# A one-core hybrid layer: low-rank decay products from the two rounded parts of x, GLA states kept in DRAM, 29 row buffers, and no head start for the RWKV pairs on TensorE

## The chip, the core and the metric

The kernel runs on one core of one Trainium2 chip. A core has TensorE (PE, matrix products), VectorE (DVE), ScalarE (ACT) and GpSimd (POOL) for elementwise work, and SyncE (SP), whose queue issues all DMAs of this kernel. The engines run their own instruction streams in order and wait for one another through semaphores. The metric is the device time of one execution in microseconds.

## What is computed

One inference step of one layer. `x` holds 1024 prompt tokens and 8 sample tokens of width 1024. One wide projection `p = x w_in` feeds three branches.

- GLA, four heads with key width 128 and value width 256. Its decay comes from a product of low rank: `a_lr` is a 16-column slice of `p`, and

```python
log_a = log_sigmoid(a_lr @ gla_alpha_w2 + gla_alpha_b) / 16
S_t = diag(a_t) S_{t-1} + k_t^T v_t ;  o_t = q_t S_t
```

- RWKV-7, sixteen heads of width 64, a recurrence with a rank-one correction per token, done in chunks of 64 tokens.
- Two sigmoid gates that weigh `o_gla @ w_up_gla` and `o_rwkv @ w_up_rwkv`. Their sum goes through `w_out`, a residual and a layer norm.

New states of both recurrences are outputs too. All inputs are fp32.

## The kernel before

**Two passes.** Prompt tokens are worked off in two halves (`PASS`). Pass 0 has 512 prompt tokens and the 8 sample tokens, as two column tiles of 260. Pass 1 has 512 tokens in one tile of 512. In each pass x is held transposed, as eight tiles of 128 rows of the width (k = 0 to 7).

**Products of three parts.** TensorE multiplies numbers of the type float32r, which are fp32 values rounded to fewer bits, faster than fp32. So x and every weight are split into a rounded part and the rounded rest: `xh`, `xl` (by `load_x`: a DMA into a row buffer, a rounding copy on ACT, a subtraction on DVE or POOL) and `whi`, `wlo` (by `load_w`). Each product of a weight block is three float32r matmuls per k: `xh whi`, `xl whi`, `xh wlo`, accumulated in one PSUM bank (`blocks`). There is one `xh` and one `xl` buffer per k, so that pass 1's parts overwrite pass 0's when the last block of pass 0 has used them.

**The low-rank product** (`low_rank`, stream kind "rank") is different: it multiplies the unrounded x rows (`raws`) by the 16 columns `wa` in fp32, with k = 0 to 7 spread over three groups of 16 output columns at 0, 32 and 64, which are added up afterwards. Raw rows are freed only when it has read them. Its result is split into three 16-row pieces of `alr` (one such tile per pass), against which `gla_head` multiplies `gw2`.

**GLA heads** (`gla_head`, kind "head"). Each works through four chunks of 128 tokens with a state `S`. Pass 0's last state of each head stays in an SBUF tile `GS` and is read by pass 1.

**RWKV pairs** (`pair`, eight per pass, kinds "pair", "turn", "chain", "norm"). The front of a pair computes decays, keys and the in-chunk matrices; a small triangular inverse is done on DVE in 31 steps, whose operand comes back from DRAM in another layout (`LD`, `Lp`, loaded as `wide<-LD`); the chain runs through 8 chunks: `pr` (`pch<-wide,gg`) to DVE (`rh`), `pu` (`pch<-rh,XT`) to ACT, `pS` (`pch<-wide`) to DVE, and so on; the norm ends it with sums over heads (`big<-part,headsr`).

**What sets the order.** Nothing is ordered at run time. A planner (class `Order`) records every operation from many coroutines: it takes, again and again, the operation with the smallest key. The key is the time at which its model lets the operation start, less a bonus: `PRIO` by stream kind off TensorE, `ON_PE` by stream kind on TensorE.

```python
key = t - (s.on_pe if s.op.eng == "P" else s.prio)
```

Where two can start at the same time, the stream with the higher `PRIO` goes first; the blocks of the projection ("block") have 0. In the model a PE operation that reads what DVE, ACT or POOL writes starts no earlier than a margin (`HOP` plus `SPARE`) after it. Each engine then executes its recorded list in order. Since one helper records every operation, all rows of the profile carry its line, L216, and are told apart by tile names. Pass 1 gets its `whi` and `wlo` back from DRAM copies (`whi<-wh`, `wlo<-wl`) through the four buffers of each kind.

**Row buffers.** 26 buffers of 128 x 520 fp32 ("row") serve x rows, projections and most temporaries.

Of the kernel before, what the change touches and what calls it, by code (L numbers as in the profile page):

```python
# [10 lines left out]
F32 = mybir.dt.float32  # L11
F32R = mybir.dt.float32r
# [8 lines left out]
P = 128  # L21
D = 1024
NK = D // P
# [12 lines left out]
NGC = HT // GC  # L36
# [8 lines left out]
HALF = HT + NS  # L45
SBUF = {
    "row": ([P, HALF], 26), "wide": ([P, 2 * HT], 4), "gg": ([P, 4 * HT], 2), "lw": ([P, HT], 2),
    "l2s": ([P, 2 * P], 1), "pc": ([P, NCH], 3), "X": ([P, 256], 1),
# [28 lines left out]
        "head": 0.3, "gate": 0.05, "w": 0.3, "out": -0.1, "state": 0, "block": 0.0}  # L77
ON_PE = {"evacuate": 0.0, "pair": 0.15, "turn": 0.1, "chain": 0.15, "norm": 0.15, "x": 0.0, "lora": 0.15, "rank": 0.1,
         "head": 0.1, "gate": 0.06, "w": 0.0, "out": -0.03, "state": 0.1, "block": 0.0}
# [64 lines left out]
def price(eng, name, out, args, ins):  # L144

    n = out.free_size()
    src = [x for x in ins if x.tensor.space != PSUM] if eng == "A" else ins
    if eng == "P":
        m = args[0].free_size()
        rows, cols = tiles(name, args)  # L150
        if name == "transpose":
            return 0.112
        if args[0].dtype == F32R:
            return max(m / 1200, n / 2200) if rows == cols == P else (m + n) / 1200
        if rows == cols == P:
            return 2 * max(m, n) / 1200 + 0.005
        return 2 * (m + n) / 1200 * rows * cols / P ** 2
# [5 lines left out]
    wide = max([n, *(x.free_size() for x in ins)]) if name in ("tensor_reduce", "bn_stats", "bn_aggr") else n  # L163
# [240 lines left out]
class Kern(Order):  # L404
# [71 lines left out]
    def setup(self):  # L476
# [80 lines left out]
    def load_constants(self):  # L557
        a, V, E = self.a, self.V, self.E
        yield from self.load("wa", self.S.dma_start(self.wa, a["wa"]))
        self.has.add("wa")  # L560
        row = yield from self.row()
        yield V.memset(row, 1.0)
        yield V.tensor_copy(self.onesr, row[:, :P])
        yield V.memset(row, 0.0)
        for t in self.alr:
            yield V.tensor_copy(t, row[0:96])
        self.has.add("alr")
        yield from self.load("pv", self.S.dma_start(self.pv, a["pv"]))
# [10 lines left out]
        yield self.S.dma_start(heads, a["heads"])  # L579
        for n in range(3):  # L580
            yield self.S.dma_start(raw[32 * n:32 * n + 16], a["gla_alpha_w2"])
        yield self.S.dma_start(self.lev, a["lev"])
# [7 lines left out]
    def load_x(self, src, i, wait=None, low_rank=False):  # L590
# [3 lines left out]
        base, n = PASS[i][:2]  # L594
        raws, his, xs, used = [], [], [], [NK]
        self.xq.append(xs)
        if low_rank:
            used = [0]
            self.spawn(self.low_rank(self.ctx[i], raws, used), "rank")

# [77 lines left out]
    def blocks(self):  # L678
        xs = None
        for b in self.plan:  # L680
# [12 lines left out]
            for tt, (t0, n) in enumerate(tiles):  # L693
# [3 lines left out]
                for k in range(NK):  # L697
# [23 lines left out]

    def low_rank(self, c, raws, used):

        ps = []
        for t0, n in c.tiles:
            ps.append((yield from self.bank("big", [P, n])))
        for k3 in range(0, NK, 3):
            ks = range(k3, min(NK, k3 + 3))
            yield lambda: len(raws) > ks[-1] and "wa" in self.has
            for (t0, n), q in zip(c.tiles, ps):  # L730
                for k in ks:
                    g = 32 * (k - k3)
                    yield self.P.matmul(q[g:g + 16], self.wa[:, 16 * k:16 * k + 16], raws[k][:, t0:t0 + n],
                                            start=(k < 3), stop=(k + 3 >= NK))
            used[0] = ks[-1] + 1
        x_ = yield from self.row(c.n)
        for (t0, n), q in zip(c.tiles, ps):
            x = x_[0:16, t0:t0 + n]
            yield self.C.copy(x, q[0:16])
            for g in (32, 64):  # L740
                yield self.V.tensor_add(x, x, q[g:g + 16])
            self.free(q)

            hi, lo, hi2 = (self.alr[c.i][g:g + 16, t0:t0 + n] for g in (0, 32, 64))
            yield lambda: "alr" in self.has
            yield self.C.copy(hi, x)
            yield self.C.copy(hi2, x)
            yield self.V.tensor_sub(lo, x, hi.bitcast(F32))
            c.alr_ready += 1
        self.free(x_)  # L750

# [18 lines left out]
    def gla_head(self, c, h, rows, g):  # L770
# [7 lines left out]
        for t0, w in c.tiles:  # L778
            pz = yield from self.bank("big", [P, w])
            yield self.P.matmul(pz, self.gw2[:, h * GDK:(h + 1) * GDK], self.alr[c.i][:, t0:t0 + w], start=True, stop=True)  # L780
            yield A.activation(z[:, t0:t0 + w], pz, AF.Identity, bias=self.pvec("gab", h))
            self.free(pz)
        yield A.activation(al, z, AF.Abs)
        yield A.activation(al, al, AF.Exp, scale=-1.0)
# [56 lines left out]

        S = self.GS[h] if c.i else None

# [11 lines left out]
        for x in range(NGC):  # L855
# [9 lines left out]
            for j in range(2):  # L865
                yield A.copy(v[j][:, s], po[:, j])
            Sn = self.GS[h] if x == NGC - 1 else (yield from self.get("S"))
            if S is not None:
                yield V.scalar_tensor_tensor(Sn, S, tot[:, x:x + 1], pS, ALU.mult, ALU.add)
                if x:  # L870
                    self.free(S)
            else:
                yield V.tensor_copy(Sn, pS)
            self.free(pb)
            S, VK = Sn, VKn
        if c.i:
            yield S_.dma_start(self.o["gla_p"][0, 0, h], S)
        else:
            yield from self.gla_sample(h, q, k, v, al, [(AT_, z), (km_, vk1)], qp_)
# [737 lines left out]
    def run_all(self):  # L1617
# [6 lines left out]
        self.ctx = [SimpleNamespace(i=i, base=b, n=n, ns=ns, tiles=t, gla_done=0, rwkv_done=0, fronts=0, lw_ready=False,  # L1624
                                    alr_ready=0, merged=0, half=0, gated=0,
                                    rg=[[] for _ in range(NPAIR)], gg=[[] for _ in range(GH)])
# [61 lines left out]
```

## Time and profile before

| what | value |
|---|---|
| median of 3 runs | 1630.18 us (1628.06 to 1632.21) |
| the profiled execution | 1629.18 us, span 1627.4 us |
| TensorE busy | 1579.8 us, 97% of the span |
| weight loads on TensorE (PEld) | 1394.6 us, 86% |
| VectorE busy | 1226.9 us, 75% |
| ScalarE busy | 844.6 us, 52% |
| GpSimd busy | 92.3 us, 6% |
| DMA | 318.42 MB, 62.9% of the 16 engines' span |

In a row of the profile stand the engine, the operation, what it writes `<-` what it reads, its shape, how often it occurs (xN), and after a bar its busy time in us and the mean of one in ns; then the idle time of the engine ahead of it and what ended that. A row of the timeline has the start and the length in us ahead of it. fp32 matmuls leave two records each, float32r matmuls one. Matmul rows overlap, since matmuls are pipelined; the distance from start to start is what one costs in a stream.

### The profile page before, as it was taken

What the parts mean: (1) busy time and instruction counts of PE and PEld (TensorE: products, weight loads), DVE (VectorE), ACT (ScalarE), POOL (GpSimd) and SP (SyncE); (2) the same over time, 40 slices, a digit from 0 to 9 for tenths busy, and PEclk for the clock granted to TensorE, in tenths of its full rate; (3) what the DMA queues carried; (4) which work ended last, traced back from release to release, by engine and by line L of the source; (5) the groups of instructions that cost most, each with busy time, mean ns of one, the idle gap of its engine ahead of it and who ended that gap; (6) DMA issues with size and microseconds to landing.
All of it is one profiled execution on the core that took longest, in us unless ns stands there. A gap on an engine that the chain in (4) does not pass through costs nothing.

```text
span 1627.4 us, 29876 instructions
## 1 busy us (share of the span) xinstructions
PE 1579.8 (97%) x10066; PEld 1394.6 (86%) x10066; DVE 1226.9 (75%) x3201; ACT 844.6 (52%) x2054; POOL 92.3 (6%) x185
## 2 busy tenths in 40 slices
PE   8999999999999999999999999999999999999998
PEld 7899999989999998788877887788788889977786
DVE  6786897788888887678677987898676784666555
ACT  5446765656566656463625472446354555554210
POOL 1100000101010000000100011100000000000000
PEclk9999999999999999999999999999999999999999
DMA  9877785696568765754465546544654487789432
GB/s 291 254 228 235 219 263 174 188 285 207 168 199 284 220 205 173 235 166 131 149 187 156 149 148 208 178 115 150 188 156 132 139 251 226 253 276 289 155 111 84
DMA packets 339572, 318.42 MB, mean 196 GB/s; under 512 B 103011, under 2 KB 225004, under 8 KB 339420
## 3 DMA queue, kind: packets, MB, share of 16 engines
q1 hardware_dynamic: 339420, 316.52, 62.9%
q8 instruction: 80, 1.31, 0.4%
q14 instruction: 72, 0.59, 0.1%
HBM read 197.55 MB, written 117.82 MB: 194 GB/s over the span
## 4 chain that ended last, share of the span: by engine, by line
PE 71%; DVE 12%; DMA 6%; SPq 4%; ACT 3%; issue 2%; POOL 0%; POOLq 0%; DVEq 0%; ACTq 0%
PE proj L216 41%; PE big L216 20%; PE pY L216 6%; SPq L216 4%; PE pch L216 4%; DVE row L216 4%; DVE X L216 2%; DVE wide L216 2%; DVE Xt L216 1%; DMA wide<-LD 1%; ACT row L216 1%; DMA wlo<-wl 1%; DVE wlo L216 1%; DMA row<-xT 1%; DMA row<-o_gla 1%
## 5 line engine op out<-in xcount | busy, mean ns | idle before, releaser
L216 PE MATMUL proj<-xh,whi 128*128 128x260 f32 (+1 forms) x1872 | 617.3, 330 | 3.8 <-DMA whi<-wh 3.1
L216 PE MATMUL proj<-xh,wlo 128*128 128x260 f32 (+1 forms) x1872 | 617.0, 330 | 1.5 <-DMA wlo<-wl 1.0
L216 PE MATMUL proj<-xl,whi 128*128 128x260 f32 (+1 forms) x1872 | 616.7, 329 | 0.0
L216 PEld LDWEIGHTS proj<-xh,whi 128*128 128x128 f32 x1872 | 355.5, 190 | 29.9 <-issue 4.6
L216 PEld LDWEIGHTS proj<-xh,wlo 128*128 128x128 f32 x1872 | 355.3, 190 | 28.7 <-issue 3.0
L216 PEld LDWEIGHTS proj<-xl,whi 128*128 128x128 f32 x1872 | 355.4, 190 | 23.3 <-issue 2.5
L216 ACT CAST whi<-wraw 128x512 fp32r<-128x512 f32 x210 | 130.0, 621 | 100.1 <-PE proj L216 51.5
L216 DVE TENSOR_TENSOR row<-row 128x512 f32<-128x512 f32 (+9 forms) x334 | 164.1, 498 | 11.7 <-ACT row L216 4.2
L216 DVE TENSOR_TENSOR wlo<-wraw,whi 128x512 fp32r<-128x512 f32 x205 | 141.3, 692 | 39.4 <-ACT whi L216 35.8
L216 ACT ACTIVATE row<-row 128x512 f32<-128x512 f32 (+4 forms) x229 | 138.1, 610 | 38.1 <-DVE row L216 28.7
L216 DVE TENSOR_TENSOR Xt<-X,wide 128x60 f32<-128x60 f32 (+24 forms) x496 | 105.1, 212 | 43.2 <-DMA wide<-LD 32.4
L216 ACT ACTIVATE row<-proj,omu 128x260 f32<-128x260 f32 (+1 forms) x99 | 54.3, 548 | 137.9 <-PE proj L216 137.2
L216 PE MATMUL big<-row 128*128 128x64 f32 (+4 forms) x712 | 115.9, 280 | 2.8 <-DVE row L216 1.8
L216 DVE TENSOR_TENSOR X<-X,Xt 128x60 f32<-128x60 f32 (+24 forms) x496 | 105.0, 212 | 12.5
L216 ACT ACTIVATE s0p<-wide,pc 64x64 f32<-64x64 f32 x256 | 87.9, 343 | 41.7 <-DVE wide L216 37.7
L216 PEld LDWEIGHTS big<-row 128*128 128x128 f32 (+1 forms) x712 | 98.1, 192 | 12.5 <-DVE row L216 4.6
L216 ACT COPY wide<-pch 64x64 f32<-64x64 f32 x216 | 44.6, 207 | 97.5 <-PE pch L216 94.2
L216 DVE SCALAR_TENSOR_TENSOR wide<-pch,pc,s0p 64x64 f32<-64x64 f32 x224 | 63.0, 281 | 42.7 <-PE pch L216 38.5
L216 DVE SCALAR_TENSOR_TENSOR row<-proj,pv,row 128x259 f32<-128x259 f32 (+1 forms) x99 | 56.4, 570 | 42.3 <-ACT tail L216 28.7
L216 ACT COPY row<-big 128x128 f32<-128x128 f32 (+7 forms) x161 | 46.0, 309 | 68.0 <-PE big L216 66.7
L216 POOL TENSOR_TENSOR row<-row 128x512 f32<-128x512 f32 (+5 forms) x35 | 38.2, 1092 | 580.7 <-ACT row L216 188.7
L216 PE MATMUL big<-az,wide 128*128 128x256 f32 x256 | 65.9, 382 | 0.3 <-ACT wide L216 0.2
(255 smaller groups left out, 2647.4 us busy)
## 6 DMA issues: line engine op xcount, KB each, us to landing
wraw<-w_in SPq DMA_DIRECT2D x146, 256.0 KB
wh<-whi SPq DMA_DIRECT2D x146, 256.0 KB
wl<-wlo SPq DMA_DIRECT2D x146, 256.0 KB
whi<-wh SPq DMA_DIRECT2D x146, 256.0 KB
wlo<-wl SPq DMA_DIRECT2D x146, 256.0 KB
wide<-LD SPq DMA_DIRECT2D x64, 128.0 KB
wraw<-w_up_gla SPq DMA_DIRECT2D x32, 256.0 KB
wraw<-w_up_rwkv SPq DMA_DIRECT2D x32, 256.0 KB
```

What stands on the lines that cost most here:

```text
L216: ways.append((eng, lambda call=call: call(out, *args, **kw), price(eng, name, out, args, ins)))
```

## The change

1. **Low-rank product.** `wa` is split once into `war`, a float32r tile with 32 columns per k: 16 of the rounded part and 16 of the rest. For each k and column tile two float32r matmuls run: `xh` against all 32 columns and `xl` against the first 16. There is one group of output columns, so the three-way addition goes. It no longer reads raw rows, which are freed as soon as `xl` is made. In pass 1 it may start only when all four heads of pass 0 have read `alr` (one tile for both passes now). `xh`, `xl` of a pass are freed by the pass's last block only once the low-rank product is recorded (`ranked`).
2. **GLA states.** `GS` is four DRAM tiles. Pass 0 writes each head's last state there, and pass 1 loads it into an `S` buffer: 4 stores and 4 loads of 128 KB more on SP.
3. **Buffers.** "row" has 29 buffers in place of 26.
4. **Planner.** `ON_PE` of "pair", "turn", "chain" and "norm" goes from 0.15, 0.1, 0.15, 0.15 to 0, and the planner's price of a float32r matmul with few columns is that of a full one.

Two constants' work differs: `gla_alpha_w2` is loaded six times instead of three, and two `alr` clearings fall away.

```diff
-    "row": ([P, HALF], 26), "wide": ([P, 2 * HT], 4), ...
+    "row": ([P, HALF], 29), "wide": ([P, 2 * HT], 4), ...
-ON_PE = {"evacuate": 0.0, "pair": 0.15, "turn": 0.1, "chain": 0.15, "norm": 0.15, "x": 0.0, ...
+ON_PE = {"evacuate": 0.0, "pair": 0.0, "turn": 0.0, "chain": 0.0, "norm": 0.0, "x": 0.0, ...
         if args[0].dtype == F32R:
-            return max(m / 1200, n / 2200) if rows == cols == P else (m + n) / 1200
+            return max(m / 1200, n / 2200) if rows == P else (m + n) / 1200
...
-        self.wa = cp.tile([P, NK * 16], F32, name="wa")
-        self.alr = [cp.tile([96, HALF], F32R, name=f"alr{n}") for n in range(2)]
+        self.war = cp.tile([P, NK * 32], F32R, name="war")
+        self.alr = cp.tile([96, HALF], F32R, name="alr")
-        self.GS = [cp.tile([P, GDV], F32, name=f"GS{h}") for h in range(GH)]
+        self.GS = [self.dr.tile([P, GDV], F32, name=f"GS{h}") for h in range(GH)]
...
+        yield V.tensor_copy(wa[:, :, 0:16], raw)
+        yield V.tensor_sub(wa[:, :, 16:32], raw, wa[:, :, 0:16].bitcast(F32))
...
-                yield lambda: used[0] > k
                 self.free(raws[k])
...
                     if fin and b.last:
+                        yield lambda: b.c.ranked
                         self.free(xh, xl)
...
-    def low_rank(self, c, raws, used):
+    def low_rank(self, c, xs):
+        yield lambda: c.i == 0 or self.ctx[0].decays == GH
         ps = []
         for t0, n in c.tiles:
             ps.append((yield from self.bank("big", [P, n])))
-        for k3 in range(0, NK, 3):
-            ks = range(k3, min(NK, k3 + 3))
-            yield lambda: len(raws) > ks[-1] and "wa" in self.has
+        for k in range(NK):
+            yield lambda: len(xs) > k and "wa" in self.has
             for (t0, n), q in zip(c.tiles, ps):
-                for k in ks:
-                    g = 32 * (k - k3)
-                    yield self.P.matmul(q[g:g + 16], self.wa[:, 16 * k:16 * k + 16], raws[k][:, t0:t0 + n],
-                                            start=(k < 3), stop=(k + 3 >= NK))
+                for x, m in list(zip(xs[k], (32, 16)))[::-1 if k else 1]:
+                    yield self.P.matmul(q[0:m], self.war[:, 32 * k:32 * k + m], x[:, t0:t0 + n],
+                                        start=(k == 0 and m == 32), stop=(k == NK - 1 and m == 32))
+        c.ranked = True
...
-        S = self.GS[h] if c.i else None
+        S = None
+        if c.i:
+            S = yield from self.get("S")
+            yield S_.dma_start(S, self.GS[h])
...
-            Sn = self.GS[h] if x == NGC - 1 else (yield from self.get("S"))
+            Sn = yield from self.get("S")
...
+        yield S_.dma_start(self.o["gla_p"][0, 0, h] if c.i else self.GS[h], S)
+        self.free(S)
```

The planner's table moves instructions on every engine. Three places are shown as they stand in the recorded lists.

**PE, pass 1, the fourth chunk of the sixth chain.** `pch<-wide,gg` is the product `pr`, whose result DVE copies to `rh`; `pch<-rh,XT` is `pu`, which waits for that copy; the `proj` rows are the projection. Before:

```order
L216 MATMUL pY<-gg,wide 128x128
L216 MATMUL pch<-wide,gg 128x128
L216 MATMUL pY<-az_177,wide 128x128
L216 MATMUL proj<-xl_9744,whi 128x512
L216 MATMUL proj<-xh_9703,wlo 128x512
L216 MATMUL proj<-xh_9712,whi 128x512
L216 MATMUL pch<-rh,XT_181 128x128
```

Now:

```order
L216 MATMUL pY<-gg,wide 128x128
L216 MATMUL pch<-wide,gg 128x128
L216 MATMUL pY<-az_176,wide 128x128
L216 MATMUL proj<-xh_9722,wlo 128x512
L216 MATMUL proj<-xh_9729,whi 128x512
L216 MATMUL proj<-xl_9731,whi 128x512
L216 MATMUL proj<-xh_9729,wlo 128x512
L216 MATMUL pch<-rh,XT_180 128x128
```

One more projection matmul stands between the two products of the chain.

**SP, pass 1, ahead of the weight block `4624`** (its first load is `whi<-wh4624_0`; `LD`, `Lp` and `wide` are the fourth pair's transfers through DRAM, `o_gla` and `sg` stores). Before:

```order
L216 DMA o_gla_90<-row_12062 128x512
L216 DMA LD13_13074<-gg_12689 32x8x32 x4
L216 DMA Lp0_184<-gg_12689 32x4x32 x4
L216 DMA wide_12688<-LD13_13074 32x1024
L216 DMA sg107_115<-row_13125 128x512
L216 DMA wide_12688<-LD13_13074 32x1024 x3
L216 DMA whi_13091<-wh4624_0_4726 128x512
L216 DMA wlo_13092<-wl4624_0_4779 128x512
```

Now:

```order
L216 DMA o_gla_90<-row_12063 128x512
L216 DMA LD13_13054<-gg_12682 32x8x32 x4
L216 DMA Lp0_183<-gg_12682 32x4x32 x4
L216 DMA wide_12681<-LD13_13054 32x1024 x4
L216 DMA whi_13088<-wh4624_0_4686 128x512
L216 DMA sg107_115<-row_13135 128x512
L216 DMA wlo_13089<-wl4624_0_4690 128x512
```

The store `sg107` stood ahead of `whi` and now stands behind it.

**PE, at the turn from pass 0 to pass 1** (blocks of 260 columns are pass 0's last, those of 512 pass 1's first; `row` is a raw x row). Before:

```order
L216 MATMUL proj_9650<-xl7_314,whi_9457 128x260
L216 MATMUL proj_9650<-xh7_285,wlo_9491 128x260
L216 MATMUL proj_9715<-xh0_9658,whi_9558 128x512
L216 MATMUL proj_9715<-xl0_9660,whi_9558 128x512
L216 MATMUL big_9266<-row_9662,wa_143 16x512
L216 MATMUL proj_9715<-xh0_9658,wlo_9559 128x512
L216 MATMUL proj_9715<-xh1_9667,whi_9558 128x512
```

Now:

```order
L216 MATMUL proj_9619<-xh4_248,wlo_9439 128x260
L216 MATMUL big_9230<-xl1_9645,war_143 16x512
L216 MATMUL big_9230<-xh1_9643,war_143 32x512
L216 MATMUL big_9230<-xl2_9654,war_143 16x512
L216 MATMUL big_9230<-xh2_9652,war_143 32x512
L216 MATMUL big_9230<-xl3_9667,war_143 16x512
L216 MATMUL big_9230<-xh3_9663,war_143 32x512
```

The low-rank matmuls of pass 1 read the split parts, and ten of the sixteen (k = 0 to 4) stand inside pass 0's last block.

More of the change, by code (lines that the diff above doesn't have):

```diff
@@ L46 @@
 SBUF = {
-    "row": ([P, HALF], 26), "wide": ([P, 2 * HT], 4), "gg": ([P, 4 * HT], 2), "lw": ([P, HT], 2),
+    "row": ([P, HALF], 29), "wide": ([P, 2 * HT], 4), "gg": ([P, 4 * HT], 2), "lw": ([P, HT], 2),
     "l2s": ([P, 2 * P], 1), "pc": ([P, NCH], 3), "X": ([P, 256], 1),
@@ L77 @@
         "head": 0.3, "gate": 0.05, "w": 0.3, "out": -0.1, "state": 0, "block": 0.0}
-ON_PE = {"evacuate": 0.0, "pair": 0.15, "turn": 0.1, "chain": 0.15, "norm": 0.15, "x": 0.0, "lora": 0.15, "rank": 0.1,
+ON_PE = {"evacuate": 0.0, "pair": 0.0, "turn": 0.0, "chain": 0.0, "norm": 0.0, "x": 0.0, "lora": 0.15, "rank": 0.1,
          "head": 0.1, "gate": 0.06, "w": 0.0, "out": -0.03, "state": 0.1, "block": 0.0}
@@ L558, in load_constants @@
         a, V, E = self.a, self.V, self.E
-        yield from self.load("wa", self.S.dma_start(self.wa, a["wa"]))
+        row = yield from self.row()
+        raw = row[:, :NK * 16]
+        yield from self.load("wa", self.S.dma_start(raw, a["wa"]))
+        wa, raw = (x.rearrange("p (k c) -> p k c", k=NK) for x in (self.war, raw))
+        yield V.tensor_copy(wa[:, :, 0:16], raw)
+        yield V.tensor_sub(wa[:, :, 16:32], raw, wa[:, :, 0:16].bitcast(F32))
         self.has.add("wa")
-        row = yield from self.row()
         yield V.memset(row, 1.0)
         yield V.tensor_copy(self.onesr, row[:, :P])
[L564 to L567, printed above, removed]
         yield from self.load("pv", self.S.dma_start(self.pv, a["pv"]))
@@ L579, in load_constants @@
         yield self.S.dma_start(heads, a["heads"])
-        for n in range(3):
-            yield self.S.dma_start(raw[32 * n:32 * n + 16], a["gla_alpha_w2"])
+        for n in range(6):
+            yield self.S.dma_start(raw[16 * n:16 * n + 16], a["gla_alpha_w2"])
         yield self.S.dma_start(self.lev, a["lev"])
@@ L726, in low_rank @@
             ps.append((yield from self.bank("big", [P, n])))
-        for k3 in range(0, NK, 3):
-            ks = range(k3, min(NK, k3 + 3))
-            yield lambda: len(raws) > ks[-1] and "wa" in self.has
+        for k in range(NK):
+            yield lambda: len(xs) > k and "wa" in self.has
             for (t0, n), q in zip(c.tiles, ps):
-                for k in ks:
-                    g = 32 * (k - k3)
-                    yield self.P.matmul(q[g:g + 16], self.wa[:, 16 * k:16 * k + 16], raws[k][:, t0:t0 + n],
-                                            start=(k < 3), stop=(k + 3 >= NK))
-            used[0] = ks[-1] + 1
-        x_ = yield from self.row(c.n)
+                for x, m in list(zip(xs[k], (32, 16)))[::-1 if k else 1]:
+                    yield self.P.matmul(q[0:m], self.war[:, 32 * k:32 * k + m], x[:, t0:t0 + n],
+                                        start=(k == 0 and m == 32), stop=(k == NK - 1 and m == 32))
+        c.ranked = True
         for (t0, n), q in zip(c.tiles, ps):
[L738 to L741, printed above, removed]
+            hi, lo, hi2 = (self.alr[g:g + 32, t0:t0 + n] for g in (0, 32, 64))
+            yield self.C.copy(hi, q[0:32])
+            yield self.C.copy(hi2, q[0:32])
+            yield self.V.tensor_sub(lo, q[0:32], hi.bitcast(F32))
             self.free(q)
[L744 to L748, printed above, removed]
             c.alr_ready += 1
-        self.free(x_)
     def landing(self, c, rows, tt):
@@ L779, in gla_head @@
             pz = yield from self.bank("big", [P, w])
-            yield self.P.matmul(pz, self.gw2[:, h * GDK:(h + 1) * GDK], self.alr[c.i][:, t0:t0 + w], start=True, stop=True)
+            yield self.P.matmul(pz, self.gw2[:, h * GDK:(h + 1) * GDK], self.alr[:, t0:t0 + w], start=True, stop=True)
             yield A.activation(z[:, t0:t0 + w], pz, AF.Identity, bias=self.pvec("gab", h))
             self.free(pz)
+        c.decays += 1
         yield A.activation(al, z, AF.Abs)
```

14 lines of the change are left out of this document (5 added, 9 removed).

## The prediction

> **What bounds the kernel now.** I read the page's busy times and the chain of waits first, then what TensorE (PE) waits for, then the timeline and the windows at the places that the change moves.
>
> ```profile
> span 1627.4 us, 29876 instructions
> PE 1579.8 (97%) x10066; PEld 1394.6 (86%) x10066; DVE 1226.9 (75%) x3201; ACT 844.6 (52%) x2054; POOL 92.3 (6%) x185
> PE 71%; DVE 12%; DMA 6%; SPq 4%; ACT 3%; issue 2%; POOL 0%; POOLq 0%; DVEq 0%; ACTq 0%
> 14.02 19.54 PE proj L216 x160
> 1435.51 5.59 PE pY L216 x24
> ```
>
> PE sets the time: it is busy in 97% of the span and holds 71% of the chain. The last two rows are unbroken stretches of the chain, and give my unit prices: 160 matmuls of 260 columns in 19.54 us are 0.122 each, 24 of 512 columns in 5.59 us are 0.233 each. Most of those 1579.8 us can't be touched, since the matmul count hardly changes. What can change is what PE loses beyond these spacings, in waits and in a lowered clock. The view of waits gives the wait on each releaser as total, times and longest:
>
> ```profile
> PE pch L216 <- DVE wide L216: 6.2, 7, 2.0
> PE pch L216 <- DVE rh L216: 4.5, 5, 1.5
> PE big L216 <- DVE part L216: 3.2, 7, 0.9
> PE proj L216 <- DMA whi<-wh: 3.1, 2, 2.5
> PE big L216 <- DMA row<-xT: 7.1, 3, 4.0
> ```
>
> The first three are short results of DVE in the RWKV chains and norms that come late; the last two are DMAs.
>
> **The sum's base.** The profiled execution took 1629.2 us, span 1627.4 and 1.8 around it. It lies 1.0 under the median of 1630.2, so I add 1.0 at the end.
>
> **A, the low-rank product of pass 1.** The pass needs eight fp32 products of 16 x 512 before and sixteen float32r ones after.
>
> ```profile
> 632.50 0.28 PE L216 MATMUL proj<-xh,wlo 128*128 128x260 f32 x1
> 632.71 1.03 PE L216 MATMUL big<-row,wa 128*16 128x512 f32 x2
> 633.67 0.49 PE L216 MATMUL pch<-rh,XT 128*128 128x128 f32 x2
> ```
>
> Start to start, one fp32 product took 0.96 (632.71 to 633.67), so eight take 7.7. Sixteen of float32r at 0.233 take 3.7. Entering the narrow product cost 0.09 (632.50 to 632.71 is 0.21 in place of the 0.12 of a 260-column row); with three or four entries that is 0.3, together 4.0: **-3.7**. No row shows float32r with a 16- or 32-column stationary. The bounds are the row of full width, 0.233, and half of the fp32 row, one of its two passes, 0.48. The second makes 7.7 and a gain of nothing. I take the first: the float32r row is of the same type and length of stream.
>
> The Trainium skill, "TensorEngine Tiling (Array Packing)", Key Properties, says that a change of tiling mode drains TensorE; that speaks against a product now strewn in more pieces. The trace has it at 0.09 an entry; some twelve entries in both passes would be 1.1 us, against about ten before, so by row and rule alike the sum keeps its value within 0.2.
>
> **B, the start.** In pass 0 the fp32 products lie in the first projection block, which waits for loads anyway.
>
> ```profile
> 9.70 0.42 PE L216 MATMUL proj<-xh,whi 128*128 128x260 f32 x1
> 9.92 0.42 PE L216 MATMUL proj<-xl,whi 128*128 128x260 f32 x1
> 11.13 1.11 PE L216 MATMUL big<-row,wa 128*16 128x260 f32 x12
> 12.18 0.39 PE L216 MATMUL proj<-xh,whi 128*128 128x260 f32 x1
> 12.97 1.05 PE L216 MATMUL big<-row,wa 128*16 128x260 f32 x6
> 13.95 0.39 PE L216 MATMUL proj<-xh,wlo 128*128 128x260 f32 x1
> 12.09 0.69 DVE L216 TENSOR_TENSOR xl<-row,xh 128x520 fp32r<-128x520 f32 x1
> ```
>
> Only 1.05 (11.13 to 12.18) and 0.98 (12.97 to 13.95) show as time, 2.0 together. Now 32 float32r products of 260 columns stand there, 3.9 at 0.122, partly at the start's slow pace of 0.22 (9.70 to 9.92). They too can fill waits, since the last `xl` is made only at 12.78. I take 3.9 less 1.1 of cover less 2.0: **+0.8**; bounds -1.5 (all covered but 0.5) and +2 (none covered).
>
> **C, the turn of the passes.** The columns of the window's row are length, then busy time and count of PE, PEld, DVE, ACT and POOL, the granted clock, the DMA share and GB/s.
>
> ```profile
> 666.00:673.00 7.00, 7.00 (x18) 3.82 (x17) 5.70 (x18) 2.38 (x5) 0.00 (x0) 0.55 0.69 259
> 665.80 1.09 PE L216 MATMUL big<-row,wa 128*16 128x512 f32 x2 [2.03 <-DMA row<-xT]
> 659.86 5.90 DMA row<-xT
> ```
>
> PE stood 2.03 us for an x row and then ran 7 us at a granted clock of 0.55, which loses 0.45 x 7 = 3.1; together 5. After the change the order shows ten low-rank matmuls of k = 0 to 4 inside pass 0's last block and the raw rows freed earlier, into three more buffers, so the x loads can start earlier. A part x7 still needs its DMA (5.90), cast and subtraction. By the order, the work on PE between the release of a buffer and the first use of its x is 6.0 to 10 us for k = 4 to 7: close, so I keep a wait of 2 without the slow clock: **-3**. Bounds: -5 (all gone) and +3 (the wait grows by the 1.4 us of cast and subtraction, and a clock loss like this one's half more).
>
> The Trainium skill, "TensorE: Matmul & The Clock Gate", Part 1, has the clock halve after an idle window of about 3.4 us. Here the granted clock fell behind a recorded wait of 2.03, and the measurement decides: by the rule a kept wait of 2 would cost only itself as it did before, C would be 0, and the sum 1620.8.
>
> **D, the chains.** Without the head start of 0.15 the products `pr` and `pu` are recorded when the model has them ready, with more of the projection between.
>
> ```profile
> 1206.71 0.39 PE L216 MATMUL pch<-wide,gg 128*128 128x128 f32 x2
> 1207.08 0.48 PE L216 MATMUL proj<-xl,whi 128*128 128x512 f32 x1
> 1208.40 0.19 DVE L216 TENSOR_TENSOR Xt<-X,wide 128x31 f32<-128x31 f32 x1 [2.27 <-DMA wide<-LD]
> 1208.62 0.29 DVE L216 COPY rh<-pch 128x128 f32<-128x128 f32 x1
> 1208.97 0.49 PE L216 MATMUL pch<-rh,XT 128*128 128x128 f32 x2 [0.95 <-DVE rh L216]
> ```
>
> This is the place that the order shows: DVE stood 2.27 us for the inverse's operand from DRAM, its copy `rh` queued behind it, and PE waited 0.95. One more matmul between (0.233) takes that much of such a wait away, not all. Over all chains, my count of the recorded lists at these spacings: `pr` to `pu` had under 1.0 us of other work in 52 of 128 steps, now in none; `pS` to the next `pr` under 1.1 us in 55 of 240, now in 13. The two rows of `pch` waits are 10.7 us; some 2 us more hides in starts that are late by less than a row shows, about 13. Ends that come from DVE standing for a DMA stay. I take some 40%: **-5**, bounds -10 (three quarters) and 0. If PE's other work is now what ends late, the price shows as longer chains, and a chain behind delays pass 1's last norms only.
>
> **E, fronts and norms.** `part` to `headsr` had under 1 us of work in 11 cases, now 3; products on `az` under 1.5 us in 26, now 10. Their waits are the `part` row, 3.2, and some 2 of smaller ones: **-2**, bounds -5 and 0.
>
> **F, a weight load behind a store.** The order on SP shows `sg107` passing from ahead of `whi` to behind it.
>
> ```profile
> 984.56 1.80 SPq L216 DMA_DIRECT2D LD<-gg  x4
> 986.40 3.26 SPq L216 DMA_DIRECT2D Lp<-gg  x4
> 990.33 0.42 SPq L216 DMA_DIRECT2D sg<-row  x1
> 992.25 0.37 SPq L216 DMA_DIRECT2D whi<-wh  x1
> 992.25 4.12 DMA whi<-wh
> 993.62 0.40 PE L216 MATMUL proj<-xh,wlo 128*128 128x512 f32 x1
> 996.50 0.47 PE L216 MATMUL proj<-xh,whi 128*128 128x512 f32 x1 [2.49 <-DMA whi<-wh]
> 996.00:1003.00 7.00, 6.50 (x21) 4.94 (x22) 5.68 (x26) 0.00 (x0) 0.00 (x0) 0.76 1.01 360
> ```
>
> The load was issued at 992.25, behind thirteen other issues, landed 4.12 later, and PE stood 2.49 and ran at 0.76 for 7 us: 0.24 x 7 = 1.7, together 4.2. After the change the weight load has 4.7 us or more of PE work between its issue and its use, more than it takes to land: **-3.5**, bounds -4.2 and 0. A planner's new order makes such places elsewhere, too; I put one half of this one against it: **+2**, bounds 0 and +6 (one such place and a half).
>
> **G, the states from DRAM.** Four stores and four loads of 128 KB are new. The stores hide, as nothing waits for them before pass 1. Each load stands on SP right behind two weight loads, whose buffers a PE matmul frees; from that matmul to the first read of `S` stand 27 to 31 matmuls of mixed size, 5.5 to 6.4 us by the spacings. The nearest DMAs have the same 128 KB:
>
> ```profile
> 181.48 4.82 DMA l2s<-lora
> 1171.64 2.60 DMA l2s<-lora
> 38.28 0.61 SPq L216 DMA_DIRECT2D l2s<-lora  x1
> 46.08 0.29 DVE L216 CAST l2p<-l2s 128x256 fp32r<-128x256 f32 x1
> ```
>
> With two issues of 0.37 ahead, a landing of 2.60 or 4.82 arrives by 3.3 to 5.6, in time; the earliest load took 7.8 to its use, and would be late by 2 to 3. DVE reads `S` and PE only its result. **+2**, bounds 0 and +22 (all four late, below).
>
> **The sum.** -3.7 + 0.8 - 3 - 5 - 2 - 3.5 + 2 + 2 = -12.4. So 1616.8 for an execution like the profiled one, and with the 1.0, **1617.8 us**.
>
> **Rivals.**
>
> *R1, the waits only change place.* The chain waits end when DVE is done, and DVE is late since it stands for `wide<-LD`, which the change leaves; the DMA waits of C and F come up at other places. For it: the 2.27 above. Against: slack grew at most edges. Left are A and B, -2.9: **1627.3**.
>
> *R2, narrow float32r products cost what an fp32 pass costs.* Then A is 0, and B is 32 x 0.24 = 7.7 in place of 3.9, +3.8: **1625.3**. For it: no row has this form. Against: the fp32 row is of another type.
>
> *R3, slower: PE stands for the `S` loads.* The states' products follow `S` at once. It decides from a landing of about 5 us; at 7.8 PE waits 7.8 + 0.7 - 6 = 2.5, and a clock as low as in C's window adds 3.1. Four times 5.6 is 22.4 in place of G's 2: **1638.2**. For it: the load at 38.28, and the DMA share of 0.69 and 1.01 in the two windows shown. Against: the 2.60 and 4.82.
>
> **How the numbers follow.** Chances: forecast 0.71, R1 0.15, R2 0.06, R3 0.08. A run of this kernel can tell about 0.3%, 4.9 us, from no change: faster means under 1625.3, slower over 1635.1. R1 counts as same, R2 lies on the line and is halved, and the forecast's own spread (D at 0, F at 0) gives 0.03 to same: faster 0.71 - 0.03 + 0.03 = 0.71, same 0.15 + 0.03 + 0.03 = 0.21, slower 0.08. The range: with D and E at their best (-8) and G at 0 the sum ends near 1606; upward it takes in R1 and R2 and ends at 1629, which leaves out R3 and the tails.
>
> **What would show it.** A: rows of `big<-xh,war` and `big<-xl,war` spaced 0.23 and 0.12 (0.48 and 0.24 is R2). C: the window behind the turn at a clock near 1. D and E: the `pch` waits near 6 and `part` near 1.5. F: no wait on `whi<-wh` at the fourth pair. G: no wait that ends with `S<-GS` on DVE with PE's behind it. The prediction is wrong if PE's busy share stays and the span does not fall, or if new waits on DMAs of over 2 us come up that drop the granted clock.

## The result, and the profile after

The changed kernel took 1610.21 us (median of 4 runs, 1608.84 to 1611.62), the kernel before 1629.12 (4 runs, 1621.84 to 1632.21): a ratio of 0.989, 95% interval 0.9856 to 0.9925. So it is 1.1% faster, 18.9 us where 12.4 was forecast, inside the range of 1606 to 1629. Timed again later, on another chip, it was 1610.46 against 1623.87 (6 and 23 runs), 0.991 (0.9888 to 0.9932), a gain of 13.4 us. The profiled executions took 1629.2 and 1610.6.

The head of the page and the chain of waits, after:

```profile
span 1608.5 us, 29899 instructions
PE 1559.6 (97%) x10066; PEld 1391.1 (86%) x10066; DVE 1226.4 (76%) x3184; ACT 836.3 (52%) x2045; POOL 104.2 (6%) x199
PE 62%; DVE 15%; DMA 10%; SPq 7%; issue 3%; ACT 3%; POOL 0%; DVEq 0%; POOLq 0%; ACTq 0%
```

TensorE (PE) is busy for 20.2 us less, and its share of the span is the same 97%. The share of the chain that runs over PE fell from 71% to 62%, that over DVE, DMA and SP's queue rose from 22% to 32%.

What PE waits for, after (total us, times, longest):

```profile
PE pch L216 <- DVE wide L216: 7.9, 8, 1.8
PE big L216 <- DVE row L216: 5.5, 6, 1.7
PE big L216 <- ACT xh L216: 5.2, 2, 4.6
PE big L216 <- DVE Xs L216: 4.5, 5, 2.2
PE pch L216 <- DVE rh L216: 2.8, 3, 1.2
PE proj L216 <- DMA wlo<-wl: 1.4, 2, 1.1
PE big L216 <- DMA S<-GS: 1.1, 2, 0.8
PE big L216 <- DVE part L216: 0.8, 1, 0.8
```

The waits have changed names, not their sum: over all rows of this view they are 37.5 us before and 40.3 after. The two `pch` rows are 10.7 us on both sides. `part` went from 3.2 to 0.8, `whi<-wh` from 3.1 to none; `big` on `Xs`, `row` and `S` came up.

Where the time went instead is seen in windows of the granted clock (columns as in the prediction: length, the five engines, clock, DMA share, GB/s). Before, two places that the prediction did not list:

```profile
355.00:365.00 10.00, 8.88 (x42) 7.79 (x43) 7.74 (x13) 7.60 (x17) 1.27 (x1) 0.66 0.74 208
1054.00:1060.00 6.00, 5.22 (x20) 4.41 (x21) 4.89 (x16) 2.22 (x6) 0.00 (x0) 0.72 0.58 182
```

After, the turn of the passes, and the only drop of that execution before its last 20 us:

```profile
656.00:663.00 7.00, 6.86 (x43) 5.17 (x44) 6.18 (x22) 4.19 (x11) 0.00 (x0) 1.00 0.92 274
663.00:670.00 7.00, 6.30 (x33) 4.92 (x32) 6.36 (x25) 3.43 (x9) 1.36 (x2) 1.00 0.59 201
925.00:935.00 10.00, 8.32 (x44) 6.88 (x43) 7.80 (x13) 5.23 (x17) 0.59 (x1) 0.83 0.15 40
```

Summed over windows of 5 us as (1 - clock) x length, up to 20 us before the end, the clock took 10.3 us before (3.4 each at 355 and 665, 1.7 each at 995 and 1055) and 1.7 after. Matmul work, counted as every matmul at its unbroken spacing, fell from 1533.5 to 1526.9, by 6.6. That count takes each matmul as if it ran alone, and for the kernel before it is too high. Its fp32 low-rank products write different groups of output columns, and where several stood together in the list they ran side by side. At the turn of the passes:

```profile
668.62 1.90 PE L216 MATMUL big<-row,wa 128*16 128x512 f32 x4
```

These four records are two products; they took 1.83 us from start to start, in the window with a granted clock of 0.55, about what one alone takes at full clock (0.96 at 632.71). By their starts, which lie within 0.01 us of the next where products ran together, the 24 products of both passes ran in 15 such sets, seven of 512 columns and eight of 260. At the spacing of one product alone (0.88 and 0.44) that is 9.7 us, where the count has 14.2 and the changed kernel needs 7.6. So TensorE's own work fell by about 2 us, not by 6.6. Of the 18.9 us between the two profiles, about 2 is matmul work, 8.6 is the clock, and some 8 is the rest: 2.8 more of waits, and some 11 less in small gaps. This says where the time lies, not yet what caused it.

### The profile page after: what moved, and what is told of

The parts are those of the page before. It is cut to its first block, busy times and chain, and to the rows that moved or that the text cites. A ratio compares the mean times of both kernels' runs of the same rounds, so it can differ in the third digit from the quotient of the medians.

```text
span 1608.5 us, 29899 instructions
## 1 busy us (share of the span) xinstructions
PE 1559.6 (97%) x10066; PEld 1391.1 (86%) x10066; DVE 1226.4 (76%) x3184; ACT 836.3 (52%) x2045; POOL 104.2 (6%) x199
## 4 chain that ended last, share of the span: by engine, by line
PE 62%; DVE 15%; DMA 10%; SPq 7%; issue 3%; ACT 3%; POOL 0%; DVEq 0%; POOLq 0%; ACTq 0%
PE proj L216 35%; PE big L216 18%; SPq L216 7%; PE pY L216 6%; DVE row L216 4%; PE pch L216 3%; DVE Xt L216 2%; DVE X L216 2%; DMA wide<-LD 2%; DVE wide L216 2%; DMA wraw<-w_in 1%; DVE wlo L216 1%; DMA Xs<-XD 1%; DVE gg L216 1%; ACT row L216 1%
## 5 line engine op out<-in xcount | busy, mean ns | idle before, releaser
L216 PEld LDWEIGHTS proj<-xl,whi 128*128 128x128 f32 x1880 | 355.7, 189 | 23.9 <-DVE xl L216 1.3
L216 DVE TENSOR_TENSOR wlo<-wraw,whi 128x512 fp32r<-128x512 f32 x205 | 141.9, 693 | 50.6 <-ACT whi L216 46.9
L216 DVE TENSOR_TENSOR row<-row 128x256 f32<-128x256 f32 (+9 forms) x317 | 159.5, 508 | 10.1 <-ACT row L216 3.1
L216 DVE TENSOR_TENSOR Xt<-X,wide 128x60 f32<-128x60 f32 (+24 forms) x496 | 107.4, 216 | 37.5 <-DMA wide<-LD 23.8
L216 DVE TENSOR_TENSOR X<-X,Xt 128x60 f32<-128x60 f32 (+24 forms) x496 | 107.3, 216 | 11.6
L216 PEld LDWEIGHTS big<-row 128*128 128x128 f32 (+1 forms) x712 | 94.4, 191 | 16.1 <-DVE row L216 9.1
L216 POOL TENSOR_TENSOR row<-row 128x512 f32<-128x512 f32 (+6 forms) x52 | 56.5, 1089 | 720.9 <-ACT row L216 218.6
L216 ACT COPY row<-big 128x128 f32<-128x128 f32 (+6 forms) x160 | 44.6, 305 | 61.3 <-PE big L216 60.3
```

The costliest lines, as they stand in the source:

```text
L216: ways.append((eng, lambda call=call: call(out, *args, **kw), price(eng, name, out, args, ins)))
```

## The experiments

The theories: **1**, the prediction's own, that each part gives its term; **2**, that what counts beyond the matmul work is how often the clock drops; **3**, that the planner's new order as a whole sets the waits, and a part's worth can't be told from it. The runs were made in four groups, each on a chip of its own beside runs of the kernel before, 66 in all, whose medians were 1623.3 to 1623.9 in each group; so ratios to before compare across groups. "Work", "waits" and "clock" are the three sums defined above, from each profile; "work" is the count of single matmuls, 3 to 4.5 us too high in the rows with 1533.5.

| kernel | median us | ratio to before, 95% | work | waits | clock |
|---|---|---|---|---|---|
| before (its first profile) | 1623.5 | 1 | 1533.5 | 37.5 | 10.3 |
| changed (again) | 1610.5 | 0.991 (0.9888 to 0.9932) | 1526.9 | 37.6 | 5.1 |
| before + ON_PE | 1634.6 | 1.0057 (1.0035 to 1.0079) | 1533.5 | 45.3 | 17.0 |
| before + low rank | 1642.2 | 1.011 (1.0085 to 1.0135) | 1526.9 | 50.2 | 17.0 |
| before + states in DRAM | 1641.9 | 1.0108 (1.0084 to 1.0133) | 1533.5 | 50.4 | 11.9 |
| changed, old ON_PE | 1645.6 | 1.0136 (1.0111 to 1.0161) | 1526.9 | 58.2 | 8.5 |
| changed, ON_PE + 0.02 | 1624.2 | 1.0 (0.9984 to 1.0016) | 1526.9 | 46.9 | 17.0 |
| before, ON_PE - 0.02 | 1638.2 | 1.0094 (1.007 to 1.0117) | 1533.5 | 48.0 | 11.9 |
| before, two places moved | 1620.1 | 0.9974 (0.996 to 0.9989) | 1533.5 | 36.0 | 5.2 |
| changed, low rank x2 | 1608.3 | 0.9904 (0.9887 to 0.9921) | 1534.5 | 30.4 | 0.0 |
| changed, x4 in pass 0 | 1613.4 | 0.9938 (0.9915 to 0.9962) | 1538.5 | 36.9 | 1.7 |
| changed, x4 in pass 1 | 1618.1 | 0.9967 (0.9942 to 0.9992) | 1538.1 | 36.1 | 3.4 |
| changed, 33 waits moved | 1638.8 | 1.0081 (1.0051 to 1.011) | 1526.9 | 55.4 | 15.4 |

### One part alone

The planner's table alone:

```diff
-ON_PE = {..., "pair": 0.15, "turn": 0.1, "chain": 0.15, "norm": 0.15, ...
+ON_PE = {..., "pair": 0.0, "turn": 0.0, "chain": 0.0, "norm": 0.0, ...
```

> The kernel before with the four ON_PE bonuses at 0 and nothing else. Theory 1 (the prediction's terms D and E: the chain and norm products wait less because more projection stands between them): about 1630 - 7 = 1623 us; the waits of pch on wide and rh fall from 10.7 us to under 7, that of big on part from 3.2 to under 1.5. Theory 2 (waits only move, and what the whole change gained beyond its low-rank product is a TensorE clock that drops less often): the sum of TensorE's waits stays within 4 us of before (about 44), and the time differs from before by no more than what (1 - granted clock) x span differs: 13 us of clock loss in the profile of before. Theory 3 (any new order of the planner moves the time by chance): anything from 1622 to 1636.

```profile
PE big L216 <- DVE Xs L216: 8.6, 4, 4.2
PE pch L216 <- DVE rh L216: 6.4, 8, 1.7
PE big L216 <- DMA row<-xT: 5.5, 2, 4.1
PE pch L216 <- DVE wide L216: 4.5, 5, 1.9
```

11 us slower, where theory 1 had 7 faster; and the waits rose by 7.8, where theory 2 allowed 4. The `pch` rows are 10.9 in sum, as before: more projection between the products did not shorten these waits. `part` did fall, to 0.2, and `big<-Xs` came up with 8.6, of which 4.2 is one wait.

The low-rank product alone (the diff of the change, without ON_PE, states and buffers):

> The kernel before with the low-rank product from the two rounded parts (one stationary of 32 columns, one alr tile, the planner's price that goes with it), 26 row buffers, states in SBUF, old ON_PE. Theory 1 (A, B, C of the prediction): -3.3 for pass 1's product, -0.6 at the start, -3 at the turn of the passes: about 1623 us, and no wait of 2 us on an x row at the turn. Theory 2: matmul work of 6.6 us less, and the rest by the clock figure: 1623.5 if the clock stays at 0.992, 1614 if it rises to 0.998. Theory 3: 1617 to 1631.

The counted matmul work fell by the 6.6, and the kernel is 19 us slower, above every range that was expected: waits of 50.2, among them 3.2 on an `xl` part at the turn that theory 1 expected to be gone.

The states alone:

> The kernel before with GLA's states in DRAM and nothing else. Theory 1 (G): +2, 1632 us, from short waits for S<-GS of about 0.5 each; rival R3 (loads land late, the clock falls): +22, 1652 us. Theory 2: waits for S<-GS under 2 us in all, the rest by the clock. Theory 3: 1624 to 1638.

```profile
PE pY L216 <- ACT xh L216: 4.7, 2, 3.5
PE big L216 <- DMA S<-GS: 4.5, 3, 2.2
```

The loads themselves cost 4.5 us of waits, above G's 2 and far from R3's 22. But the kernel lost 18, more than theories 1 and 3 allowed, mostly at places that have nothing to do with the states, such as 3.5 us at the first output projection. In the changed kernel's profiles `S<-GS` stands with 1.1 and 3.5.

The changed kernel with the old ON_PE:

```diff
-ON_PE = {..., "pair": 0.0, "turn": 0.0, "chain": 0.0, "norm": 0.0, ...
+ON_PE = {..., "pair": 0.15, "turn": 0.1, "chain": 0.15, "norm": 0.15, ...
```

> The changed kernel with the old ON_PE bonuses (0.15, 0.1, 0.15, 0.15); all else as changed. Theory 1: 1610 + 7 = 1617 us, with the pch waits not below those of the changed kernel (10.7) and part's wait up to 3. Theory 2: the time follows the clock figure: 1610 with 0.998, 1620 with 0.992, and TensorE's waits within 4 us of 44. Theory 3: 1604 to 1618.

35 us slower than the changed kernel, five times theory 1's price and above all three ranges. One wait at the first output projection (`pY` on `xh`) alone took 6.87 us. Theory 1's terms don't add: ON_PE alone costs 11 on one side and its removal 35 on the other.

### The same kernel again, and a neutral shift

> The changed kernel, unchanged, on the chip of this series, with the granted clock of every run. Theory 2 (run to run the time of one kernel moves with the clock alone): its runs lie on a line of 1.6 us for each 0.001 of clock, at 0.995 to 0.998, 1606 to 1613 us. If the clock does not explain the runs, they scatter without it.

Here the clock of each run was seen. Over the 66 runs of before a straight line gives 1.65 us per 0.001 of clock, about the span times 0.001, with a correlation of 0.76; the six of the changed kernel give 1.7. The mean clock is 0.9935 before and 0.9967 in these six: about 5 of the 13 us between these medians. One wait shows how it comes about. The same product, in the two profiles of the changed kernel, first as in the result and then again:

```profile
403.81 0.46 PE L216 MATMUL pch<-wide,gg 128*128 128x128 f32 x2 [1.75 <-DVE wide L216]
403.00:410.00 7.00, 6.19 (x51) 6.06 (x52) 6.81 (x29) 2.22 (x9) 0.00 (x0) 1.00 0.61 205
```

```profile
403.12 0.46 PE L216 MATMUL pch<-wide,gg 128*128 128x128 f32 x2 [1.85 <-DVE wide L216]
403.00:410.00 7.00, 6.88 (x46) 6.92 (x47) 5.96 (x24) 1.40 (x5) 0.00 (x0) 0.76 0.53 179
```

A wait of 1.75 left the clock at 1.00, one of 1.85 at the same place cost 0.24 x 7 = 1.7 us more. The Trainium skill, "TensorE: Matmul & The Clock Gate", Part 1, says that the gate looks at a window of about 3.4 us that runs freely, so that its effect varies from run to run. The losses here agree in size: 1.7 is 3.4 us at half speed, 3.4 twice that. That a whole idle window is needed does not agree: waits of 1.85 to 2.5 were enough, and so, at 355 in the kernel before, were three waits of 0.64, 0.55 and 0.84 within four us (and 0.65, 0.54 and 0.84 at the same place in the kernel with two places moved, below).

The changed kernel with 0.02 in place of 0:

```diff
-ON_PE = {..., "pair": 0.0, "turn": 0.0, "chain": 0.0, "norm": 0.0, ...
+ON_PE = {..., "pair": 0.02, "turn": 0.02, "chain": 0.02, "norm": 0.02, ...
```

> The changed kernel with the four ON_PE bonuses at 0.02 in place of 0: the same computation, the same buffers, a slightly other rule for ties. Theory 1 (the gain comes from the parts of the change): 1610, within 3 us of the changed kernel. Theory 3 (a new order moves the time by chance, as the four runs before suggest, each of which lost 11 to 22 us where gains of 7 or a loss of 2 were expected): a time 5 to 30 us above the changed kernel, with the same matmul work and other waits.

All that theory 1 credits to the four parts is still in this kernel, and the whole gain is gone: 1624.2, the time of before. Its waits:

```profile
PE pch L216 <- DVE wide L216: 5.2, 5, 2.1
PE pch L216 <- DVE rh L216: 4.8, 7, 2.1
PE big L216 <- ACT xh L216: 4.7, 1, 4.7
PE big L216 <- ACT part L216: 4.7, 1, 4.7
PE big L216 <- DVE part L216: 4.0, 3, 2.4
```

Single waits of 4.7 and 2.4 on `part` stand where the changed kernel has one of 0.8; 7 to 9 us more of waits and 12 to 15 of clock than in the two profiles of the changed kernel. This profile is the slowest of the twelve runs, 5 us above their median, so it shows more than the usual loss.

The counterpart on the kernel before (0.13, 0.08, 0.13, 0.13 for 0.15, 0.1, 0.15, 0.15):

> The kernel before with its four ON_PE bonuses lower by 0.02 (0.13, 0.08, 0.13, 0.13), nothing else: the counterpart of the neutral shift of the changed kernel, which cost 14 us there. If both kernels stand at a good point of the planner's rule and any step off it costs: 5 to 20 us slower than before, 1629 to 1644. If only the changed kernel's order is a lucky one and that of before a middling one: within 6 us of before, or faster. In both cases matmul work as before and the difference in the waits and the clock.

15 us slower, with waits of 48.0. Each of the six kernels with an order that the planner made anew (these two, and the four with a part) lost 11 to 35 us against the kernel it departs from. So, as far as six neighbours can tell, both kernels stand at good points of the planner's rule. Two good points differ by 13 to 19 us; what a part is worth under an order of its own can't be read from a kernel in which the order is made again.

### The order frozen

For the next five the order was taken out of the planner: a table holds which stream's operation is recorded next and on which engine, and the loop follows it. In the traces the kernel with the doubled products below has the changed kernel's instructions in the same order on every engine but for the doubled matmuls, and the kernel with two places moved differs from before at these places alone. (The helper's line is then L222.)

```diff
-            best, before = None, list(self.streams)
...
+        for n in range(0, len(todo), 2):
+            key = names[todo[n] + 256 * todo[n + 1]]
...
+            s = [s for s in self.streams if s.key == key[:-1] and s.op is not None][0]
```

The kernel before, two places moved (rows of the table for SP and PE, and raw rows freed by a stream of their own):

```diff
 SP:  wide<-LD  x1
-SP:  sg107<-row
 SP:  wide<-LD  x3
 SP:  whi, wlo, whi, wlo, whi, wlo
+SP:  sg107<-row
...
-PE:  big<-row,wa  (k = 4; then 5 and 6)
 PE:  proj<-xh,wlo ... proj<-xh4,wlo
+PE:  big<-row,wa  (k = 4, 5, 6)
```

> The kernel before with its recorded order frozen, and two places moved: on SP the store sg107 stands behind the six loads of weights that followed it (F), and on TensorE the three low-rank products at the turn of the passes stand eleven or more matmuls later, so that none waits for its x row (C). Theory 1 (C and F are lost for good where they stand): no wait of 2 us at 666 and 996, the clock at 1 behind both, 5.5 + 4.2 = about 9 us less than before. Rival: what is saved there is waited for a little later, since DVE and the DMAs are no earlier: 0 to 3 us less.

```profile
667.63 0.50 PE L222 MATMUL proj<-xh,whi 128*128 128x512 f32 x1 [0.41 <-ACT xh L222]
668.35 0.50 PE L222 MATMUL proj<-xl,whi 128*128 128x512 f32 x1 [0.23 <-DVE xl L222]
668.78 1.03 PE L222 MATMUL big<-row,wa 128*16 128x512 f32 x2
990.11 0.47 PE L222 MATMUL proj<-xh,whi 128*128 128x512 f32 x1 [1.05 <-DMA whi<-wh]
666.00:673.00 7.00, 6.36 (x25) 2.99 (x24) 5.01 (x16) 3.13 (x6) 0.00 (x0) 1.00 1.01 382
989.00:996.00 7.00, 5.72 (x24) 4.02 (x24) 5.63 (x26) 0.74 (x2) 0.00 (x0) 1.00 1.02 334
```

At their places both waits went as expected: no wait on an x row, 1.05 in place of 2.49 on `whi`, and the clock at 1.00 in both windows. From ten projection products ahead of pass 1's first one to twenty behind it, PE needed 6.2 us more than its own matmuls before and 1.4 here (products side by side counted once). The span of its profile is 1620.6, 6.8 less than the one profile of before; in the median the kernel gained 3.8 us (0.26%, 0.11 to 0.40). The 9 were reckoned from an execution in which both waits had also met a drop of the clock; the waits alone, 2.0 and 1.4 of 2.5, are 3.4. So the x row and the store are shown as the causes of the waits at these two places, in one profile of each kernel. The gain of 1.8 to 6.5 us excludes the 9 of theory 1; the rival's upper end, 3, lies inside it, so that a part of what was saved may be waited for later. How often the clock falls behind them in other executions was not measured.

Every low-rank matmul twice (shortened, in the form that the x4 kernels below have, with `times` = 2):

```diff
-                    yield self.P.matmul(q[0:m], self.war[...], x[...], start=..., stop=...)
+                    ops = [self.P.matmul(q[0:m], self.war[...], x[...], start=..., stop=...) for r in range(times)]
+                    (recorded as one operation)
```

> The changed kernel with its recorded order frozen and every low-rank matmul issued twice in a row (the decays are computed from twice the product, so their values are not the reference's; everything else is as it was). Theory (A and B: a narrow float32r product costs its stream, 0.233 and 0.12): 16 x 0.233 + 32 x 0.12 = 3.7 + 3.9, of which 0.5 to 1.5 hides at the start: +6 to +7.6 us over the changed kernel. Rival: short products hide in waits that TensorE has anyway: +2 or less. Rival: a longer order upsets the rest: over +10.

```profile
PE big L222 <- ACT xh L222: 4.6, 1, 4.6
PE pch L222 <- DVE wide L222: 3.7, 6, 0.8
PE big L222 <- DVE row L222: 2.9, 5, 1.3
PE big L222 <- DMA S<-GS: 2.8, 2, 1.7
PE pch L222 <- DVE rh L222: 2.5, 2, 1.3
```

7.6 us more of matmul work, and no more time (1608.3; by the two intervals, 1 us less, uncertain by some 4.5). The theory's +6 to +7.6 failed. The `pch` wait on `wide` fell from 7.9 and 7.1 in the changed kernel's profiles to 3.7, all waits from 40.3 and 37.6 to 30.4, in a profile that is the fastest of its six runs. This fits that DVE and ACT go on while PE does more early work, so that their results are there when PE asks. It also suggests that the low-rank work which the change took away explains little of the gain by itself. Two kernels tried to part the effect by place:

> The changed kernel's frozen order, every low-rank matmul of pass 0 issued four times in a row (the decays of pass 0 come from four times the product, so those values are not the reference's). 96 matmuls of 260 columns more at 0.12 to 0.22: 11.5 us or more of work ahead of the first blocks. If TensorE's work adds to the time: 1610 + 10 to 13 = 1621. If what TensorE is given early comes back as fewer waits, since DVE, ACT and the DMAs run on meanwhile (the doubling cost nothing): 1605 to 1614, with TensorE's waits 8 us or more below those of the changed kernel (37.6 and 40.3).

> The same frozen order, every low-rank matmul of pass 1 four times (the decays of pass 1 are not the reference's): 48 matmuls of 512 columns more, 11.2 us at the turn of the passes. Work adds: 1621. Work at this place comes back as fewer waits behind it: 1607 to 1614. If only early work comes back (a head start of DVE that lasts through the program), this one costs its 11 and the one of pass 0 nothing.

11.6 us more work in pass 0 cost 0.28% against the changed kernel, 4.5 us; 11.2 us in pass 1 cost 0.57%, 9.2 us; each is uncertain by some 5, worked out from the two intervals. For early work, then, anything from none to some 80% may stay, for work at the turn some 40% to all of it: the medians alone do not part the two places. Nor did the waits fall by the 8 us that the first expectation set as its sign: they are 36.9 and 36.1, against 37.6 and 40.3. The spans of the two profiles are both some 6 us above the changed kernel's, about half of the added work.

Last, the waits themselves. 33 products on which PE stood over 0.4 us in both profiles were moved behind as much work of the other streams:

```diff
 (for each: stream s, product p, PE waits w)
-PE:  p of s
 PE:  ... other streams' products worth w + 0.3 us
+PE:  p of s, with the operations of s that stood between
```

> The changed kernel's order frozen, and 33 products on which TensorE waited over 0.4 us in both of its profiles (33 us of waits in all, the weight loads' waits not among them) stand later, each behind so much of the other streams' TensorE work as it waited, and 0.3 us more; the operations of its stream that stood in that stretch go with it. Everything is computed. If a wait is lost time that other work can fill: 20 to 30 us less, 1582 to 1592, clock 0.998 or more. If the time is set by the chains and the streams' other engines, so that a wait filled here comes back at the next product of the same stream: 1605 to 1615, waits again near 38.

28 us slower than the changed kernel, outside both ranges. One chain, in the changed kernel and then here:

```profile
874.24 0.38 PE L216 MATMUL pch<-wide 128*128 128x128 f32 x2
877.78 0.46 PE L216 MATMUL pch<-wide,gg 128*128 128x128 f32 x2 [1.53 <-DVE wide L216]
878.88 0.29 DVE L216 COPY rh<-pch 128x128 f32<-128x128 f32 x1
879.23 0.48 PE L216 MATMUL pch<-rh,XT 128*128 128x128 f32 x2
```

```profile
881.32 0.38 PE L222 MATMUL pch<-wide 128*128 128x128 f32 x2
885.24 0.38 PE L222 MATMUL pch<-wide,gg 128*128 128x128 f32 x2
885.53 0.21 DVE L222 TENSOR_TENSOR Xt<-X,wide 128x50 f32<-128x50 f32 x1
887.82 0.29 DVE L222 COPY rh<-pch 128x128 f32<-128x128 f32 x1
888.16 0.49 PE L222 MATMUL pch<-rh,XT 128*128 128x128 f32 x2 [2.31 <-DVE rh L222]
889.23 0.49 PE L222 MATMUL pch<-wide 128*128 128x128 f32 x2 [0.58 <-ACT wide L222]
```

The wait of 1.53 on `wide` was filled, and the next product of the same chain, which stayed at its place in the list, waited 2.31 for `rh`, and the one behind it 0.58. The row `pch` on `rh` grew from 2.8 to 15.3 us. Counted in order, the `pch` products show this everywhere. Eleven waited over 0.4 us in the changed kernel's first profile; none of them does here. At all eleven places the next `pch` product of the list waits over 0.4 us instead, 13.7 us in all where it was 10.7.

Two things in the run make these waits. The projection matmuls that stood between the two products (four in this chain) were used up ahead of the first, so nothing was left in front of the second. And the operations that went with a product include the copy to `rh`: in this chain it stands nine inverse steps later on DVE (885.53 to 887.82), and comes 2.6 us behind its product's start, where it came 1.1 behind. So it is at seven of the eleven places, by four to eleven instructions of DVE. These copies came 5.2 us later in sum, of the 11.2 us that the seven products waited. That part is the run's own making. So the run shows that these waits came back at the next link when they were filled in this way; what filling one is worth with DVE's order kept and with other work left for the next link, it does not show. The moves that gave time were a store and products that no chain hung on.

## Why the prediction was right, and where it was not

- **The result** (1617.8 forecast, 1610.2 measured) was of the sign and within the range, at one and a half times the size; against the later runs the gain is 13.4, close to the 12.4. That closeness is in good part luck: D and E, 7 of the 12.4, did not come in the sum, and what came in their place, fewer drops of the clock at places not listed and fewer small gaps, was not in the forecast. The range's own lower end is 1607.8 by its terms (8 and 2 below 1617.8), not 1606.
- **A, -3.7.** The sixteen products of pass 1 take 4.4 us by their spacings, among them 0.5 that holds a wait, in place of the forecast's 7.7. But two of the eight products before ran side by side (the row at 668.62 above), so there were seven places of 0.96, 6.7 us: A was -2.3 at full clock, and mis-sized by 1.4. R2's price of 0.48 is refuted by rows of the kind

```profile
659.06 0.39 PE L216 MATMUL big<-xl,war 128*16 128x512 f32 x1
659.29 0.39 PE L216 MATMUL big<-xh,war 128*32 128x512 f32 x1
659.51 0.40 PE L216 MATMUL big<-xl,war 128*16 128x512 f32 x1
```

  at 0.23 from start to start, full and narrow alike. How much of A counts as time is open: the x4 run in pass 1 allows some 40% to all of it, the doubling at most half of the work of both passes.
- **B, +0.8.** PE reached the 96th projection product at 23.1 and 23.9 us in two profiles, against 23.8 before: between -0.7 and +0.1. Of 11.6 us added at this place 4.5 stayed, uncertain by 5 (the x4 run of pass 0); the term had counted all that its cover did not hide.
- **C, -3.** What PE lost at the turn beyond its own matmuls, over the thirty projection products named above, went from 6.2 to 2.4 and 2.9 in two profiles, by a little more than the 3 of the forecast, and the clock stood at 1.00 there. Right in size; the moved products of the frozen order show that the wait came from the x row.
- **D, -5.** Failed. The `pch` rows are 10.7 us before, 10.7 and 10.5 after, 10.9 with ON_PE alone. The step that failed is to price "one more matmul between takes that much of such a wait away" over the products that waited, with all others as they were. Counted in order, ten `pch` products waited over 0.4 us before and eleven after, and only two are the same. Eight waits are gone, among them the 0.95 that the forecast showed; nine came at products that had none of that length, such as 1.75 at 403.81, and eight of these nine waited over 0.4 us in the second profile too. Why the new order makes just these late is not shown.
- **E, -2.** `part` fell by 2.4 as forecast, with ON_PE alone too. In the sum it was paid back by `Xs`, 0.9 to 4.5, and `row`, 1.8 to 5.5. R1 was right about the waits: 37.5 before, 40.3 and 37.6 after.
- **F, -3.5, and +2 for new places.** The waits on `whi<-wh`, 3.1, are gone; those on `wlo<-wl` went from one of 1.0 to two of 1.4 in all. In the frozen order the moved store took 1.4 of the 2.5 us at this place.
- **G, +2.** 1.1 and 3.5 us in two profiles. R3 did not happen: the longest single wait for a load in them is 1.6. The waits are PE's own, at `big<-row,S`, which reads `S` itself; the forecast had DVE between.
- **What was missing** is the clock as a term of its own. The sum had 4.8 of the 10.3 us that it cost before (C and F) and left out 355 and 1055. The gain of 8.6 here is partly a matter of which executions were profiled: by the mean clock of many runs it is some 5. The small gaps, the largest share of the rest, no run explains.
- **What the forecast could not know** is how far the order alone moves the time. Its range was made of the terms; six orders that differ little from these two lie 11 to 35 us above them, and none of the terms says so.

What stays open: why this order loses less to the clock and to small gaps than its neighbours. No run separates the low-rank product, the states and the 29 buffers under a fixed order, since each changes the list of operations or where they may stand; 29 buffers alone, and the changed kernel without them, were not tried.

## What to carry to other kernels

Where a planner makes the order, a neutral shift of its table (here 0.02 us of a bonus) comes first: it gives the spread against which a part's gain has to stand, here 14 us. To learn what one place costs, freeze the order and move that place alone. A wait on a load or behind a store could be taken away here; eleven waits inside dependent chains, filled where they showed, came back at the next product, and the kernel got slower; in that run the copies between two products had moved as well, so it does not show that such a wait can't be filled.

## What was not expected of the hardware

Run to run, this kernel moves by 1.65 us for each 0.001 of the mean granted clock (66 runs, 0.989 to 0.996, 1616.6 to 1632.1 us): 58% of the variance of an unchanged program (its standard deviation of 3.3 us falls to 2.1 about that line) goes with how often the clock drops. And 7.6 us of added matmuls cost nothing measurable, within some 4.5 us, on an engine that is busy in 97% of the span.
